# Second SwiGLU of a decoder block: its norm's column sums and broadcast at fixed places, its sums behind the row splits, the gate stage's tiles placed anew

## The chip, the cores and the metric

The kernel runs on one core of one Trainium2 chip. The metric is the device time of one execution in microseconds (us), taken as the median of several runs. A second execution of the same program carries a hardware profile; all rows below come from that one.

The engines are named as the profile names them: PE is TensorE's matmul, PEld its weight load, DVE is VectorE, ACT ScalarE, POOL GpSimd, SP SyncE. L126 is line 126 of the kernel.

## What is computed

One layer of a decoder block on 512 tokens of width 1024. The part that matters here is its end:

```python
h = h + o                                                  # attention + S5, through w_out
h = h + 0.5 * swiglu(rmsnorm(h, norm_ffn2), ffn2_w1, ffn2_w3, ffn2_w2)
gate = sigmoid(rmsnorm(h, norm_ple) @ w_ple_gate)
h = h + gate * (p @ w_ple)                                 # p: 512 x 256, the per-layer embedding
return rmsnorm(h, norm_final)

def swiglu(x, w1, w3, w2): return (silu(x @ w1) * (x @ w3)) @ w2      # d_ff = 2816
def rmsnorm(x, g): return x * rsqrt(mean(x * x, -1) + 1e-6) * g
```

## The kernel before

The state `h` stands with features on the partitions, as a tile of 128 partitions, 8 feature tiles k, 512 tokens. Every large product is made in a reduced float format from split operands: a weight w becomes `hi` (a cast on ACT, L147) and `lo` (raw minus hi, on DVE, L149), an activation likewise `xh` and `xl`, and `mm3` issues three matmuls, hi with xh, hi with xl, lo with xh. Weights come in units of 128 x 1024 (512 KB): `unit()` starts the load on ACT's DMA queue into a ring of four `raw` tiles, and ring places for three `hi` and three `lo` follow. PSUM has four tags A, B, C, D (rows call them ps_A to ps_D) of two banks each; a matmul has to wait until the bank that it writes has been read.

Most of the order of instructions is set by a scheduler, which simulates the program and issues what it thinks will be ready. Two things bind it: `pinned(...)` keeps the marked instructions in the order in which the program gives them, and `tc.issue_after(x)` lets the instructions in its block be placed only behind x. Whatever is left is placed by the scheduler's own simulation. Each engine then works strictly in its order: an instruction that waits holds up everything behind it on that engine.

**From the attention's end to the second SwiGLU.** When `h` is complete, its squares have been added up in `acc` (L183, DVE). The embedding's products p @ w_ple follow on PE: eight feature tiles m, two k tiles each, three matmuls each, 48 in all (rows ps_B<-ph,hi, pl,hi and ph,lo); ACT copies each result (`et`, L1272), and it goes to DRAM for the gate stage. Among these products `rsqrt_rows` makes the norm's factor. Four narrow matmuls sum `acc` over the features (row ps_D<-ones,acc), DVE and POOL work out the reciprocal root (`ms`, `nt`, `ri`, and `dg`, L260 to L267), and one matmul broadcasts it over the partitions (row ps_D<-dg,ones). Only then can `Scaled.spread` make the SwiGLU's input: for each feature tile k, DVE scales the row (`xn`, L218), ACT casts it (`xh`, L219) and DVE subtracts (`xl`, L225). These DVE instructions are pinned among each other. Of the 48 products just the first is pinned, and the sums, the broadcast and the other products stand where the scheduler put them.

**The SwiGLU.** Hidden tiles f are made in turn by `up(f)`. The first two (N_PLAIN = 2), f = 0 and 1, take plain products of 8 k tiles with two weights (j = 0 writes bank A, j = 1 bank B): 2 x 8 x 3 matmuls of 128 x 512 each. From f = 2 on `up_fast` uses a scheme with seven products for eight, of 128 x 256 matmuls, and for it `combine` (in `spread`) makes four sums of quarters of the scaled rows, t1, t2, t4 and t3: two additions on DVE each (L234, rows xn<-xn), a cast on ACT (`sh`, L237), a subtraction on DVE (`sl`, L238). These sums are not pinned and not bound to the splits. The weights of `up_fast` are sums too (`s`, L309 to L316, DVE).

**The gate stage.** After the SwiGLU's last feature tile of `h` (L398) its split and square follow (`xh` L173 and `sq` L182 on ACT, `xl` L174 and `acc` L183 on DVE). The stage goes through the tokens in two halves of 256 and in each through m = 0 to 7, with 24 matmuls of 128 x 256 for each m. Behind m = 0 of the first half come the column sums of `ng.finish`, later the broadcast, a copy of it (`rb`, L192), and with that the first result is scaled (`gt`, L1307); m = 4 needs the bank that the first `gt` reads. The stage's pool `gp` holds the embedding `ple` read back from DRAM, five kept weights `hi` and `lo`, and small tiles. Its tiles share their place in memory with those of the SwiGLU that are freed at its end, so what a gate tile has to wait for depends on where in the pool it lies. `PADS[2]` is a filling of 192 bytes ahead of the tiles that follow.

Of the kernel before, what the change touches and what calls it, by code (L numbers as in the profile page):

```python
# [10 lines left out]
F32 = mybir.dt.float32  # L11
# [8 lines left out]
SEQ = 512  # L20
PLE_DIM = 256
D_FF = 2816
KT = D_MODEL // 128
# [53 lines left out]
def block_kernel(ctx: ExitStack, tc: tile.TileContext, a: dict, out: bass.AP):  # L77
# [73 lines left out]

    def mm3(o, wh, wl, xh, xl, first, last, pin=False):
        p = mm(o, wh, xh, first, False)
        if pin:
            pinned(p)
        mm(o, wh, xl, False, False)
        mm(o, wl, xh, False, last)
        return p

# [34 lines left out]
    class Scaled(Norm):  # L194
# [13 lines left out]
        def spread(self, tmp, xpool, pool, pb):  # L208
# [22 lines left out]
            def combine(n, a, b, op):  # L231
                t = tmp().rearrange("p a (b c) -> p (a b) c", c=256)
                for i in range(2):
                    V.tensor_tensor(t[:, 2 * i:2 * i + 2], a(i), b(i), op)  # L234
                hi = pool.tile([128, 4, 256], FR, name=f"sh{n}")
                lo = pool.tile([128, 4, 256], FR, name=f"sl{n}")
                S.copy(hi, t)  # L237
                V.tensor_tensor(lo, t, hi.bitcast(F32), OP.subtract)  # L238
                return (hi, lo), lambda i: t[:, 2 * i:2 * i + 2]
# [11 lines left out]
    def rsqrt_rows(parts, nb, pin=False):  # L251

        st = bank("D", (128, 4))[:, :nb]
        for b in range(nb):
# [11 lines left out]
        for b in range(nb):  # L266
            V.tensor_scalar(dg[:, b, :], ident, ri[:, b:b + 1], None, OP.mult)  # L267
        pb = bank("D")[:, :nb * 128]
        mm(pb, ones, dg.rearrange("p b t -> p (b t)"), True, True)
        return ri, pb  # L270

# [8 lines left out]
    def ffn(nrm, done, bg=None, first=None, fast=None):  # L280
        wait = next(bg) if bg else None
        with ExitStack() as fctx:
# [74 lines left out]
            def up(f):  # L357
# [6 lines left out]
                if after:  # L364
                    both = [(j, k) for k0 in (0, 4) for j in range(2) for k in range(k0, k0 + 4)]
                for j, k in both:
# [294 lines left out]
    first = unit()  # L661
# [596 lines left out]
    pled = dram.tile([D_MODEL, SEQ], F32, tag="pled", name="pled")  # L1258
    wu = None
    for m in range(KT):  # L1260
# [3 lines left out]
        for k in range(2):  # L1264
            q = (m * 2 + k) % 8
            sl = slice(q * 128, (q + 1) * 128)
            with tc.issue_after(lead.ins) if m + k else nullcontext():
                p = mm3(o, wu[0][:, sl], wu[1][:, sl], ph[:, k], pls[k], k == 0, k == 1, pin=m + k == 0)
            if m + k == 0:
                lead = p  # L1270
        et = fp2.tile([128, SEQ], F32, tag=("t1", "t3")[m % 2], name="et")
        S.copy(et, o)  # L1272
        nc.sync.dma_start(pled[128 * m:128 * m + 128], et)
        if m == 0:
            _, pb2 = rsqrt_rows([n2.acc], 4)
            n2.spread(lambda: hp2.tile([128, 2, SEQ], F32, tag="hq", name="xn"), xpool, x2pool, pb2)
    ffn(n2, feed_next(3), fast=(hp2, fp2))
# [3 lines left out]
    ng = state["n"]  # L1281
    with tc.tile_pool(name="gate", bufs=2, reuse_waits="tile") as gp:
        ple = gp.tile([128, KT, SEQ], F32, tag="ple", name="ple", bufs=1)
        for m in range(KT):
            nc.sync.dma_start(ple[:, m], pled[128 * m:128 * m + 128])
        gf = gp.tile([128, KT], F32, tag="gf", name="gf", bufs=1)
        pad(gp, PADS[2])
        nc.scalar.dma_start(gf, a["gain_f"])
        acc = npool.tile([128, SEQ], F32, tag="acc", name="accf", bufs=1)
        ov = out.rearrange("(k p) t -> p k t", p=128)  # L1290
        HS = SEQ // 2
        gate_w = []
        for hf in range(2):
            cs = slice(hf * HS, hf * HS + HS)
            for i in range(KT):
                m = i if hf == 0 else KT - 1 - i
                if hf == 0:
                    gate_w.append(unit(keep=gp if m < KT - 3 else None))
# [25 lines left out]

N_PLAIN = 2
XSHIFT = 224
FILL = 5
# [10 lines left out]
DEBUG_STOP = None  # L1338
PADS = 320, 0, 192

# [144 lines left out]
```

## Time and profile before

| | us |
|---|---|
| median of 3 runs | 1105.64 |
| lowest, highest | 1103.83, 1106.86 |
| the profiled execution | 1106.72 |
| its span, first to last instruction | 1104.9 |
| PE busy in it | 1054.1 (95%) |
| DVE busy | 776.7 (70%) |
| ACT busy | 462.7 (42%) |
| mean granted clock of TensorE, share of full | 0.973 |

The busy times are sums over the whole span. A row of the timeline gives the start and the length of an instruction; matmuls overlap, so their pace is read from the distance of their starts. A bracket at a row's end is the idle time of that engine just before it, and who ended it. The chain of waits follows the work that ended last back from the end and tells which engine held it for which share.

### The profile page before, as it was taken

To read this page: it belongs to the slowest core of one execution; us is meant where nothing else is said; L and a number is where in the kernel's file an instruction comes from. 1 tells how busy PE (TensorE), PEld (TensorE's weight loads), DVE (VectorE), ACT (ScalarE), POOL (GpSimd) and SP (SyncE) were. 2 spreads that over 40 slices of the span, in tenths; PEclk is the share of its full clock that TensorE was granted. 3 is DMA by queue.
4 is the path that set the end of the run, shared out by engine and by line. 5 is a ranking of instruction groups with operands and counts; after the bars stand their busy time and mean duration, and the time that the engine had idled before them with its cause. 6 is when DMAs were issued, how large, how long until landed. Compare 5 with 4: busy or idle time off the path is not lost.

```text
span 1104.9 us, 15111 instructions
## 1 busy us (share of the span) xinstructions
PE 1054.1 (95%) x5854; PEld 888.6 (80%) x5854; DVE 776.7 (70%) x1328; ACT 462.7 (42%) x786; POOL 164.0 (15%) x187
## 2 busy tenths in 40 slices
PE   7999999999999998888899999899999999999896
PEld 5888888888888887665577667699899899898795
DVE  6995446445447755779688976897598678687766
ACT  6222223124123422236758865455256246255431
POOL 4006146335538100000000000000000000000000
PEclk9999999999999998989799999899999999999898
DMA  7332325327635836557121013233333323325302
GB/s 250 117 114 96 96 96 153 104 94 173 164 96 152 261 113 169 180 173 254 38 71 39 1 39 133 95 96 115 96 97 104 126 80 107 119 77 162 124 2 77
DMA packets 48596, 128.48 MB, mean 116 GB/s; under 512 B 10300, under 2 KB 17052, under 8 KB 47500
## 3 DMA queue, kind: packets, MB, share of 16 engines
q10 hardware_dynamic: 26080, 90.51, 25.6%
q0 software_dynamic: 4336, 17.60, 6.1%
q1 hardware_dynamic: 18108, 19.40, 5.6%
q8 instruction: 46, 0.75, 0.3%
q14 instruction: 26, 0.21, 0.1%
HBM read 111.99 MB, written 15.73 MB: 116 GB/s over the span
## 4 chain that ended last, share of the span: by engine, by line
PE 77%; DVE 8%; DMA 6%; ACT 4%; issue 4%; POOL 0%; SPq 0%; ACTq 0%; POOLq 0%; DVEq 0%
PE ps_C L126 23%; PE ps_A L126 23%; PE ps_B L126 21%; PE ps_D L126 10%; DVE lo L149 1%; DMA kf<-kd 1%; DMA kd<-r 1%; DMA kcd<-ra 1%; DMA qd<-r 1%; DMA qf<-qd 1%; ACT e L737 1%; ACT eh L737 1%; DMA dk<-in_s_dT 1%; DMA cst<-vcd 1%; ACT ps_B L737 1%
## 5 line engine op out<-in xcount | busy, mean ns | idle before, releaser
L147 ACT CAST hi<-raw 128x1024 fp32r<-128x1024 f32 (+2 forms) x148 | 153.7, 1041 | 339.6 <-PE ps_C L126 121.7
L149 DVE TENSOR_TENSOR lo<-raw,hi 128x1024 fp32r<-128x1024 f32 (+2 forms) x148 | 191.0, 1293 | 57.2 <-ACT hi L147 56.5
L126 PE MATMUL ps_C<-hq,hi 128*128 128x512 f32 x704 | 217.2, 390 | 0.7 <-DVE h L398 0.7
L126 PEld LDWEIGHTS ps_C<-hq,hi 128*128 128x128 f32 x704 | 131.4, 188 | 28.2 <-DVE h L398 1.5
L126 PE MATMUL ps_A<-xh,hi 128*128 128x512 f32 (+1 forms) x376 | 133.5, 356 | 9.6 <-ACT xh L173 6.2
L126 PE MATMUL ps_A<-xl,hi 128*128 128x512 f32 (+1 forms) x376 | 133.9, 356 | 5.3 <-DVE xl L225 5.0
L126 PE MATMUL ps_C<-hq,lo 128*128 128x512 f32 x352 | 137.0, 389 | 0.0
L126 PE MATMUL ps_A<-xh,lo 128*128 128x512 f32 (+1 forms) x376 | 132.9, 353 | 0.0
L126 PE MATMUL ps_B<-xh,lo 128*128 128x512 f32 (+1 forms) x280 | 105.2, 376 | 3.7 <-DVE lo L149 3.7
L126 PE MATMUL ps_B<-xh,hi 128*128 128x512 f32 (+1 forms) x280 | 104.8, 374 | 0.1
L126 PE MATMUL ps_B<-xl,hi 128*128 128x512 f32 (+1 forms) x280 | 104.3, 373 | 0.0
L261 POOL TENSOR_TENSOR ri<-ms,negh 128x4 f32<-128x4 f32 (+1 forms) x6 | 5.5, 921 | 594.0 <-DVE ms L260 594.0
L126 PEld LDWEIGHTS ps_A<-xh,hi 128*128 128x128 f32 x376 | 72.5, 193 | 20.4 <-ACT xh L173 6.2
L126 PEld LDWEIGHTS ps_A<-xl,hi 128*128 128x128 f32 x376 | 72.6, 193 | 18.1 <-DVE xl L225 7.7
L398 DVE SCALAR_TENSOR_TENSOR h<-ps_C,h 128x512 f32<-128x512 f32 x64 | 43.9, 689 | 57.2 <-PE ps_C L126 57.0
L147 ACT CAST hi<-s 128x1024 fp32r<-128x1024 f32 x40 | 42.1, 1052 | 92.0 <-PE ps_D L126 39.7
L126 PEld LDWEIGHTS ps_A<-xh,lo 128*128 128x128 f32 x376 | 72.6, 193 | 9.0
L126 PEld LDWEIGHTS ps_C<-hq,lo 128*128 128x128 f32 x352 | 66.1, 188 | 13.7
L126 PEld LDWEIGHTS ps_B<-xh,lo 128*128 128x128 f32 x280 | 54.0, 193 | 13.8 <-DVE lo L149 4.8
L126 PEld LDWEIGHTS ps_B<-xh,hi 128*128 128x128 f32 x280 | 54.1, 193 | 9.6 <-issue 0.5
L149 DVE TENSOR_TENSOR lo<-s,hi 128x1024 fp32r<-128x1024 f32 x40 | 49.0, 1226 | 18.0 <-ACT hi L147 17.9
L126 PEld LDWEIGHTS ps_B<-xl,hi 128*128 128x128 f32 x280 | 54.0, 193 | 9.2 <-issue 0.2
(402 smaller groups left out, 2327.2 us busy)
## 6 DMA issues: line engine op xcount, KB each, us to landing
raw<-in_wpack ACTq DMA_DIRECT2D x168, 512.0 KB, 3.6
sc<-s5d POOLq DMA_DIRECT2D x8, 1024.0 KB, 6.9
raw<-in_wpack SPq DMA_DIRECT2D x4, 512.0 KB, 8.1
h<-in_xT SPq DMA_DIRECT2D x8, 256.0 KB, 4.5
s5d<-fs POOLq DMA_DIRECT2D x1, 2048.0 KB, 11.7
s5d<-gt POOLq DMA_DIRECT2D x1, 2048.0 KB, 12.2
s5d<-tcs POOLq DMA_DIRECT2D x2, 1024.0 KB, 9.5
qf<-qd SPq DMA_DIRECT2D x16, 128.0 KB, 4.4
```

What stands on the lines that cost most here:

```text
L126: return PE.matmul(o, lhsT, rhs, start=start, stop=stop, **kw)
L147: S.copy(hi[:, c], raw[:, c])
L149: V.tensor_tensor(lo[:, c], raw[:, c], hi[:, c].bitcast(F32), OP.subtract)
L261: G.tensor_tensor(ri, ms, negh[:, :nb], OP.pow)
L398: V.scalar_tensor_tensor(h[:, m, :], o, 0.5, h[:, m, :], OP.mult, OP.add)
L737: S.activation(*args, **kw)
```

## The change

It has four parts.

First, all 48 embedding products are pinned, one behind the other, and `rsqrt_rows` is cut in two (`rsqrt_steps`, a generator): the sums with the arithmetic behind them, and the broadcast. `NORM_AT` places the first behind product pair (m, k) = (2, 0), the second behind (4, 1); both matmul groups are pinned in the same row of instructions as the products.

Second, the additions of `combine` are issued only behind the last `xl`.

Third, the products of f = 0 go through k on the outside and j on the inside, where they went through two halves of k with j between.

Fourth, in the gate stage's pool the weights of m = 0 are allocated first, then `gf`, a filling of 24,832 bytes, and then `ple`; `PADS[2]` is 224.

The number of instructions of each engine is the same.

```diff
             def combine(n, a, b, op):
                 t = tmp().rearrange("p a (b c) -> p (a b) c", c=256)
-                for i in range(2):
-                    V.tensor_tensor(t[:, 2 * i:2 * i + 2], a(i), b(i), op)
+                with tc.issue_after(self.last.ins):
+                    for i in range(2):
+                        V.tensor_tensor(t[:, 2 * i:2 * i + 2], a(i), b(i), op)
...
     def rsqrt_rows(parts, nb, pin=False):
+        steps = rsqrt_steps(parts, nb, pin)
+        next(steps)
+        return next(steps)
+
+    def rsqrt_steps(parts, nb, pin=False, pin_last=False):
...
+        yield
         pb = bank("D")[:, :nb * 128]
-        mm(pb, ones, dg.rearrange("p b t -> p (b t)"), True, True)
-        return ri, pb
+        p = mm(pb, ones, dg.rearrange("p b t -> p (b t)"), True, True)
+        if pin_last:
+            pinned(p)
+        yield ri, pb
...
                 if after:
-                    both = [(j, k) for k0 in (0, 4) for j in range(2) for k in range(k0, k0 + 4)]
+                    both = [(j, k) for k in range(KT) for j in range(2)]
...
+    norm2 = rsqrt_steps([n2.acc], 4, True, True)
...
-            with tc.issue_after(lead.ins) if m + k else nullcontext():
-                p = mm3(o, wu[0][:, sl], wu[1][:, sl], ph[:, k], pls[k], k == 0, k == 1, pin=m + k == 0)
-            if m + k == 0:
-                lead = p
+            for i, (w_, x_) in enumerate(((wu[0], ph[:, k]), (wu[0], pls[k]), (wu[1], ph[:, k]))):
+                pinned(mm(o, w_[:, sl], x_, k + i == 0, k == 1 and i == 2))
+            if (m, k) == NORM_AT[0]:
+                next(norm2)
+            if (m, k) == NORM_AT[1]:
+                _, pb2 = next(norm2)
+                n2.spread(lambda: hp2.tile([128, 2, SEQ], F32, tag="hq", name="xn"), xpool, x2pool, pb2)
...
-        if m == 0:
-            _, pb2 = rsqrt_rows([n2.acc], 4)
-            n2.spread(lambda: hp2.tile([128, 2, SEQ], F32, tag="hq", name="xn"), xpool, x2pool, pb2)
...
     with tc.tile_pool(name="gate", bufs=2, reuse_waits="tile") as gp:
+        pad(gp, PADS[2])
+        gate_w = [unit(keep=gp)]
+        gf = gp.tile([128, KT], F32, tag="gf", name="gf", bufs=1)
+        gp.tile([128, PADS[3] // 4], F32, name="gpad", bufs=1)
         ple = gp.tile([128, KT, SEQ], F32, tag="ple", name="ple", bufs=1)
...
-        gf = gp.tile([128, KT], F32, tag="gf", name="gf", bufs=1)
-        pad(gp, PADS[2])
...
-        gate_w = []
...
-                if hf == 0:
+                if hf == 0 and m:
                     gate_w.append(unit(keep=gp if m < KT - 3 else None))
...
+NORM_AT = (2, 0), (4, 1)
...
-PADS = 320, 0, 192
+PADS = 320, 0, 224, 24832
```

What the built programs show of it follows for three places; the lines' numbers have moved by a few between the two kernels.

PE, among the embedding's products (ps_B<-ph and <-pl). The difference has two pieces here, one ahead of the sums and one ahead of the broadcast, with three products taken away in each; the piece at the broadcast reads:

```order
 L126 MATMUL ps_B<-pl,hi 128x512
 L126 MATMUL ps_B<-ph,lo 128x512
-L126 MATMUL ps_B<-ph,hi 128x512
-L126 MATMUL ps_B<-pl,hi 128x512
-L126 MATMUL ps_B<-ph,lo 128x512
 L126 MATMUL ps_D<-dg,ones 128x512
 L126 MATMUL ps_B<-ph,hi 128x512
```

The broadcast stands behind 30 products now and stood behind 36; the sums stand behind 15 and stood behind 18.

DVE, at the row splits of the second SwiGLU, before (`xn<-h` scales a row, `xl` is its split, `xn<-xn` are combine's additions, `sl` its subtraction, `lo<-raw,hi` a weight's split):

```order
L225 TENSOR_TENSOR xl<-xn,xh 128x512
L218 SCALAR_TENSOR_TENSOR xn<-h,gains,ps_D 128x512
L234 TENSOR_TENSOR xn<-xn 128x512 x2
L225 TENSOR_TENSOR xl<-xn,xh 128x512
L218 SCALAR_TENSOR_TENSOR xn<-h,gains,ps_D 128x512
L234 TENSOR_TENSOR xn<-xn 128x512
L225 TENSOR_TENSOR xl<-xn,xh 128x512
L238 TENSOR_TENSOR sl<-xn,sh 128x1024
L234 TENSOR_TENSOR xn<-xn 128x512 x2
L225 TENSOR_TENSOR xl<-xn,xh 128x512
L149 TENSOR_TENSOR lo<-raw,hi 128x1024 x2
```

The same place now, on from the fifth split:

```order
L222 TENSOR_TENSOR xl<-xn,xh 128x512
L215 SCALAR_TENSOR_TENSOR xn<-h,gains,ps_D 128x512
L222 TENSOR_TENSOR xl<-xn,xh 128x512
L215 SCALAR_TENSOR_TENSOR xn<-h,gains,ps_D 128x512
L222 TENSOR_TENSOR xl<-xn,xh 128x512 x2
L232 TENSOR_TENSOR xn<-xn 128x512 x2
L149 TENSOR_TENSOR lo<-raw,hi 128x1024 x2
L232 TENSOR_TENSOR xn<-xn 128x512 x2
L149 TENSOR_TENSOR lo<-raw,hi 128x1024
L236 TENSOR_TENSOR sl<-xn,sh 128x1024
```

Five additions and one subtraction went from between the splits to behind the last one; two additions and then two weight splits stand there first.

ACT, at the change from the SwiGLU to the gate stage, before (`xh` and `sq` are of the last feature tiles of h, `hi` the gate weights' casts):

```order
L173 ACTIVATE xh<-h,gains 128x512
L182 ACTIVATE sq<-h 128x512
L1288 DMA gf<-in_gain_f 128x8
L173 ACTIVATE xh<-h,gains 128x512
L182 ACTIVATE sq<-h 128x512
L147 CAST hi<-raw 128x1024 x4
```

And now:

```order
L170 ACTIVATE xh<-h,gains 128x512
L179 ACTIVATE sq<-h 128x512
L147 CAST hi<-raw 128x1024
L1297 DMA gf<-in_gain_f 128x8
L170 ACTIVATE xh<-h,gains 128x512
L179 ACTIVATE sq<-h 128x512
L147 CAST hi<-raw 128x1024 x3
```

One cast went ahead of the last `xh` and `sq`. On DVE the `lo` that belongs to it went ahead of the last `xl` and `acc` in the same way.

## Rows read from the trace of the kernel before

**Rows 1.** The profile's page: the span, the busy times of PE, and the chain of waits by engine.

```profile
span 1104.9 us, 15111 instructions
...
PE 1054.1 (95%) x5854; PEld 888.6 (80%) x5854; DVE 776.7 (70%) x1328; ACT 462.7 (42%) x786; POOL 164.0 (15%) x187
...
PE 77%; DVE 8%; DMA 6%; ACT 4%; issue 4%; POOL 0%; SPq 0%; ACTq 0%; POOLq 0%; DVEq 0%
```

**Rows 2.** The waits of PE, from 660 to 720 us (the norm and the first hidden tiles of the second SwiGLU): engine and what it worked on, whom it waited for, us in total, times, the longest.

```profile
PE ps_A L126 <- DVE xl L225: 5.0, 5, 2.0
```

**Rows 3.** Busy time by windows: the row splits, and a stretch of the SwiGLU later. Columns: window, its length, busy us of each engine (with the number of instructions), TensorE's granted clock as a share of full, DMA share, GB/s.

```profile
685.00:699.00 14.00, 8.93 (x30) 5.09 (x29) 13.43 (x21) 7.68 (x11) 0.00 (x0) 0.93 0.10 38
900.00:1000.00 100.00, 100.00 (x735) 95.20 (x735) 80.43 (x117) 46.60 (x76) 0.00 (x0) 1.00 0.35 107
```

**Rows 4.** The timeline of DVE from 671 to 713 us: start, length, line, operation, what it writes and reads.

```profile
674.02 0.68 DVE L183 TENSOR_TENSOR acc<-acc,sq 128x512 f32<-128x512 f32 x1
...
678.87 0.88 DVE L267 TENSOR_SCALAR dg<-ident,ri 128x128 f32<-128x128 f32 x4
682.38 1.41 DVE L218 SCALAR_TENSOR_TENSOR xn<-h,gains,ps_D 128x512 f32<-128x512 f32 x2 [2.63 <-PE ps_D L126]
...
689.52 0.69 DVE L225 TENSOR_TENSOR xl<-xn,xh 128x512 fp32r<-128x512 f32 x1
...
690.78 1.29 DVE L234 TENSOR_TENSOR xn<-xn 128x512 f32<-128x512 f32 x2
...
693.25 0.69 DVE L234 TENSOR_TENSOR xn<-xn 128x512 f32<-128x512 f32 x1
...
694.45 1.22 DVE L238 TENSOR_TENSOR sl<-xn,sh 128x1024 fp32r<-128x1024 f32 x1
695.58 1.29 DVE L234 TENSOR_TENSOR xn<-xn 128x512 f32<-128x512 f32 x2
696.79 0.69 DVE L225 TENSOR_TENSOR xl<-xn,xh 128x512 fp32r<-128x512 f32 x1
697.39 2.36 DVE L149 TENSOR_TENSOR lo<-raw,hi 128x1024 fp32r<-128x1024 f32 x2
```

**Rows 5.** The timeline of ACT in the same stretch.

```profile
684.91 1.05 ACT L147 CAST hi<-raw 128x1024 fp32r<-128x1024 f32 x1
...
686.34 1.14 ACT L219 CAST xh<-xn 128x512 fp32r<-128x512 f32 x2
```

**Rows 6.** The timeline of PE from the embedding's products to the first 128 x 256 product of `up_fast`.

```profile
675.29 0.39 PE L126 MATMUL ps_B<-ph,hi 128*128 128x512 f32 x1
...
675.98 0.95 PE L126 MATMUL ps_D<-ones,acc 128*128 128x1 f32 x8
...
679.42 0.39 PE L126 MATMUL ps_B<-ph,lo 128*128 128x512 f32 x1
...
681.32 1.02 PE L126 MATMUL ps_D<-dg,ones 128*128 128x512 f32 x2
...
692.73 0.50 PE L126 MATMUL ps_A<-xl,hi 128*128 128x512 f32 x1 [1.49 <-DVE xl L225]
...
697.53 0.80 PE L126 MATMUL ps_A<-xl,hi 128*128 128x512 f32 x1 [1.98 <-DVE xl L225]
698.12 0.63 PE L126 MATMUL ps_A<-xh,lo 128*128 128x512 f32 x1
...
703.95 0.41 PE L126 MATMUL ps_B<-xh,lo 128*128 128x512 f32 x1
...
716.69 0.28 PE L126 MATMUL ps_A<-xh,hi 128*128 128x256 f32 x1
```

**Rows 7.** Busy time by windows of 2 us from the last row split on, columns as in rows 3.

```profile
696.00:698.00 2.00, 0.47 (x1) 0.47 (x2) 2.00 (x4) 1.05 (x1) 0.00 (x0) 0.79 0.00 0
698.00:700.00 2.00, 2.00 (x5) 1.18 (x5) 2.00 (x3) 1.62 (x2) 0.00 (x0) 0.50 0.22 33
```

**Rows 8.** The timeline of PE at the gate stage.

```profile
1039.45 0.58 PE L126 MATMUL ps_A<-xh,hi 128*128 128x256 f32 x1 [2.99 <-ACT hi L147]
...
1045.53 0.95 PE L126 MATMUL ps_D<-ones,acc 128*128 128x1 f32 x8
...
1053.54 1.02 PE L126 MATMUL ps_D<-dg,ones 128*128 128x512 f32 x2
...
1055.90 0.36 PE L126 MATMUL ps_A<-xh,hi 128*128 128x256 f32 x1 [0.28 <-DVE gt L1307]
```

**Rows 9.** The timeline of DVE at the gate stage.

```profile
1036.49 0.69 DVE L398 SCALAR_TENSOR_TENSOR h<-ps_C,h 128x512 f32<-128x512 f32 x1 [0.56 <-PE ps_C L126]
...
1039.43 4.63 DVE L149 TENSOR_TENSOR lo<-raw,hi 128x1024 fp32r<-128x1024 f32 x4
...
1054.60 0.69 DVE L192 COPY rb<-ps_D 128x512 f32<-128x512 f32 x1 [2.18 <-PE ps_D L126]
```

**Rows 10.** The timeline of ACT at the gate stage.

```profile
1034.45 0.62 ACT L182 ACTIVATE sq<-h 128x512 f32<-128x512 f32 x1
...
1038.37 2.93 ACT L147 CAST hi<-raw 128x1024 fp32r<-128x1024 f32 x3
```

**Rows 11.** Busy time by a window of 2 us at the gate stage's start, columns as in rows 3.

```profile
1038.00:1040.00 2.00, 0.55 (x2) 0.50 (x2) 1.90 (x3) 2.00 (x3) 0.00 (x0) 0.62 0.00 0
```

**Rows 12.** DMA issues from 690 to 715 us: what, queue, count, KB each, median us from issue to landing.

```profile
raw<-in_wpack ACTq DMA_DIRECT2D x5, 512.0 KB, 3.7
```

More of the change, by code (lines that the diff above doesn't have):

```diff
@@ L150, in split, with mm3 @@
         return hi, lo
[L152 to L155, printed above, removed]
+    def mm3(o, wh, wl, xh, xl, first, last):
+        mm(o, wh, xh, first, False)
         mm(o, wh, xl, False, False)
         mm(o, wl, xh, False, last)
-        return p
     xpool = ctx.enter_context(tc.tile_pool(name="xpool", bufs=1))
@@ L1258, in block_kernel @@
     pled = dram.tile([D_MODEL, SEQ], F32, tag="pled", name="pled")
-    wu = None
+    norm2 = rsqrt_steps([n2.acc], 4, True, True)
     for m in range(KT):
```

## The prediction

> **What bounds the kernel now.** I read the page first. PE is busy for 1054.1 of 1104.9 us and holds 77% of the chain of waits [rows 1]; so the kernel can only gain where PE waits or where it runs slowly. The profiled execution took 1106.72 us, 1.8 us more than its span, and lies 0.1% over the median of 1105.64; I work on its rows and take the difference off the median.
>
> Second, PE's waits around the change. From 660 to 720 us there are five waits for a row split `xl`, 5.0 us together [rows 2]. The window of the splits shows why: from 685 to 699 us DVE works 13.43 of 14.00 us and PE only 8.93 [rows 3]. DVE is the bound there. Later in the SwiGLU the same row view has PE full and DVE at 80% [rows 3]: there, time won at the start is kept, and DVE work put off from the splits finds room. A difference under 0.3%, 3.3 us, can hardly be told from none.
>
> Third, the granted clock. PE waits 1.98 us for the last split, after a stretch in which it was about half busy [rows 3, 6]. [...] The products from 698.12 to 703.95 run in 13 steps of 0.448 us, against 0.2275 in the 56 steps from 703.95 to 716.69 [rows 6]. The slow stretch costs 13 x 0.22 = **2.9 us**. The gate stage has the same picture: PE idles 2.99 us for a weight cast [rows 8], the clock is 0.62 from 1038 to 1040 [rows 11], and 26 products take 6.08 us up to the column sums at 1045.53 [rows 8].
>
> **Part 1, sums and broadcast.** Three products are 675.98 - 675.29 = 0.69 us [rows 6]; the sums start that much earlier, at 675.29. `acc` is complete at 674.02 + 0.68 = 674.70 [rows 4], so no wait is added. The chain through DVE and POOL ended with `dg` at 678.87 + 0.88 = 679.75 [rows 4] and ends now at 679.06. The broadcast's new place, behind 30 products, comes up at 679.42 + 0.23 = 679.65 [rows 6], 0.6 us later than `dg`: PE does not wait, and queued behind it would only be products that nobody awaits soon. It stood at 681.32, so it comes **1.67 us** earlier, and the first scaled row starts at 680.71, not at 682.38 [rows 4]. The embedding's results are needed only in the gate stage, 350 us later; that six products come after the broadcast costs nothing, since PE works through the same 48 in the same time. SP's and POOL's queues keep their order.
>
> **Part 2, the sums of quarters.** Between the splits DVE did five additions and one subtraction. By the distance to the next row's start, a pair of additions took 696.79 - 695.58 = 1.21 us, the subtraction 695.58 - 694.45 = 1.13 [rows 4]: 5 x 0.60 + 1.13 = **4.1 us** leave the path. One thing is late next: ACT's weight cast at 684.91 waits for the embedding's last product, whose time does not move, and the fourth `xh` stands behind it and a copy, at 686.34 [rows 5]. So the fourth split cannot start before about 686.95, where its turn would be at 685.9: about 1.0 us is lost, of which 0.5 had been lost before. From there, at a pace of 1.26 (689.52 to 690.78 [rows 4]), splits five to seven start at 688.21, 689.47 and 690.73, the eighth at 691.47; it ends at 692.16. It ended at 696.79 + 0.69 = 697.48 [rows 4]: **-5.3 us**, which agrees with -1.7 - 4.1 + 0.5.
>
> **Part 3, the loop order, and PE behind the splits.** With j inside, each split feeds six products of f = 0 instead of three as soon as both weights are there, so PE has more to do between splits. Its waits for splits four to six come to 0.4, 0.5 and 0.5 us in the replay. Behind the last split two new ones arise, because the two additions now stand ahead of the weight splits on DVE (they were 697.39, directly behind the last split [rows 4]): a weight's `lo` is done at 694.6, for which PE waits 0.4 us, and PE waits 1.1 us for a cast `hi` whose place in the ring comes free late. Both are bounded by 0 and by the whole pair of additions with a cast, 1.2 + 1.05 = 2.3 us [rows 4, 5]; I take **+1.5**, the replay's own value. No single wait in it comes near the 1.98 or 2.99 us after which the clock fell, and the half-busy stretch is half as long; I therefore count the 2.9 us of slow clock as gone. Sum for the norm: -5.3 - 2.9 + 1.5 = **-6.7 us**; the first 128 x 256 product moves from 716.69 to about 710.0.
>
> [...]
>
> **Part 4, the gate stage.** The cast of m = 0 now stands ahead of the last `xh` and `sq` on ACT; it starts when the square before is done, 1034.45 + 0.62 = 1035.07 [rows 10], and ends at 1036.1. Its `lo` follows the last `h` on DVE, 1036.49 + 0.60 = 1037.09 [rows 9], and ends at 1038.3. PE can do its first two products at once, then waits about 1.7 us for `lo`, and goes on at 1038.38 where it went on at 1039.45 [rows 8]. If the clock stays up, 24 products at the full pace follow. That pace is (1053.54 - 1045.53 - 0.81) / 61 = 0.118 us for the 61 products between sums and broadcast [rows 8]; 0.81 is the time the sums take up. So the sums start at 1041.2 instead of 1045.53, **-4.3 us**: 1.1 from the earlier start, 0.2 from two products done earlier, 3.0 from the clock. The last `xl` and `acc` move back by one `lo`, 1.2 us; `acc` is ready at 1039.5, before it is needed. The broadcast stands behind three products fewer: 1041.2 + 0.81 + 58 x 0.118 = 1048.85 against 1053.54 [rows 8]. Then one step is lost again. `rb` follows 1.06 later, as before (1054.60 [rows 9]), at 1049.9, but one `lo` (4.63 / 4 = 1.16 us a piece [rows 9]) now stands on DVE between it and the first `gt`, so `gt` starts at 1051.7 and m = 4 on PE at 1052.2, with a wait of 1.1 us where it had 0.28. It started at 1055.90 [rows 8]: **-3.7 us**. From there on both kernels run the same rows.
>
> **Sum.** -6.7 - 3.7 = -10.4 us: the profiled execution would be 1096.3, the median **1095.2**. With no new wait behind the splits (-1.5) and none at `gt` (-1.1) it is 1092.6.
>
> **The rivals.** (a) The clock falls all the same. For it: PE is only half to two thirds busy from 684 to 692 us, and at the gate a wait of 1.7 us stands close to the 1.98 that was followed by a fall. Against it: in 685 to 699 the mean clock was still 0.93 although PE worked 8.93 of 14 us, so half-busy alone did not bring it down [rows 3], and a wait of 1.49 us passed without a fall [rows 6]. At the norm it costs 2.9 (1098.1), at the gate 2.7 (1097.9; 3.0 for the products, less what the wait at `gt` takes up), at both 1100.8.
>
> (b) The put-off sums come too late. DVE has no idle time between 692 and about 711 us in my replay: six more rows of it lie behind the splits, and the first weight sum of `up_fast` needs a load that lands 3.7 us after issue [rows 12]. The third subtraction is ready at 710.3, PE needs it at 713.2: 2.9 us of slack. A missed ring place costs one landing and one cast, 3.7 + 1.05, less the slack: 2 to 3 us, or about 1098.
>
> (c) The gate's cast gets no earlier, since its place in memory still has a reader among the last products. Then only the norm counts: 1098.9.
>
> (d) Slower. The same queue of DVE work as in (b) at one place, the sums for f = 2: PE stops there until the last one is made. It decides from a lateness of 2.9 + 10.4 = 13.3 us on, that is two to three loads missed one behind the other at 4.75 each beyond the slack; over 1109 it needs 16.6. DVE's 80% in the later window [rows 3] speaks against any such pile-up.
>
> **How the numbers follow.** Forecast 0.66; (a) 0.17; (b) 0.09; (c) 0.06; (d) 0.02. The predicted time is the forecast's, 1095. The range goes from 1092, where none of the new waits arises, to 1101, where the clock falls at both places; outside lie (d) and combinations of (a) to (c), under 2 in 10. Faster by more than 3.3 us: all of the forecast and nearly all of (a) to (c), 0.93; within: 0.05, combinations; slower: 0.02.
>
> **What would show it.** In the profile after: the broadcast at about 679.7 with no wait ahead of it on PE; eight `xl` rows on DVE with no addition between them, the last ending near 692; no stretch of clock 0.50 between 690 and 705; the first 128 x 256 product near 710. At the gate: one weight cast ahead of the last `xh`, sums some 11 us earlier than 1045.53, the clock at 1.00. I am wrong if the clock falls, if PE has a new wait for `sl`, `sh` or `s` near 703 to 715, or if DVE becomes the bound over the first products of `up_fast`.

## The result and the profile after

The changed kernel takes 1092.87 us in the median of 4 runs (1090.99 to 1096.34), before 1106.13 on the same chip (4 runs, 1103.83 to 1106.86): 13.3 us less. The ratio of the two means is 0.9887, with a 95% interval from 0.9856 to 0.9918: 1.13% or 12.5 us less, at least 9.1 and at most 15.9. Predicted were 1095 and a range from 1092 to 1101.

The profile page of the changed kernel has the span, the busy times and the chain of waits in the lines that answer to [rows 1]:

```profile
span 1089.1 us, 15119 instructions
...
PE 1042.0 (96%) x5854; PEld 881.4 (81%) x5854; DVE 775.2 (71%) x1328; ACT 462.1 (42%) x786; POOL 163.9 (15%) x187
...
PE 78%; DVE 8%; DMA 5%; issue 4%; ACT 4%; SPq 0%; POOLq 0%; POOL 0%; ACTq 0%; DVEq 0%
```

The profiled execution is 15.8 us shorter in its span. This is not yet the change's work: the stretches have to be cut out. Two marks that both traces have are the embedding's first product on PE and the first 128 x 256 product of the second SwiGLU; I call the time between their starts the norm's segment. A second pair is the last 128 x 512 product of the SwiGLU (ps_C) and the first product of m = 4, which is the first one on bank A behind the broadcast; the time between these I call the gate segment.

PE's timeline of the changed kernel, norm's segment:

```profile
666.51 0.39 PE L126 MATMUL ps_B<-ph,hi 128*128 128x512 f32 x1
...
669.98 0.95 PE L126 MATMUL ps_D<-ones,acc 128*128 128x1 f32 x8
...
674.35 1.02 PE L126 MATMUL ps_D<-dg,ones 128*128 128x512 f32 x2
...
686.18 0.50 PE L126 MATMUL ps_A<-xl,hi 128*128 128x512 f32 x1 [0.30 <-DVE xl L222]
...
688.60 0.50 PE L126 MATMUL ps_B<-xh,hi 128*128 128x512 f32 x1 [0.90 <-ACT hi L147]
...
689.29 0.50 PE L126 MATMUL ps_B<-xh,lo 128*128 128x512 f32 x1
...
704.38 0.28 PE L126 MATMUL ps_A<-xh,hi 128*128 128x256 f32 x1
```

The norm's segment is 704.38 - 666.51 = **37.87 us** here, and it was 716.69 - 671.82 = 44.87 before, 671.82 being the start of that product in the trace of before: 7.00 us less. The sums stand 3.47 us behind the start, where they stood 4.16; the broadcast 7.84, where it stood 9.50 [rows 6]. No bracket stands at either, so neither had to be waited for. DVE's timeline of the same stretch:

```profile
675.41 1.41 DVE L215 SCALAR_TENSOR_TENSOR xn<-h,gains,ps_D 128x512 f32<-128x512 f32 x2 [1.66 <-PE ps_D L126]
...
681.65 0.69 DVE L222 TENSOR_TENSOR xl<-xn,xh 128x512 fp32r<-128x512 f32 x1 [0.94 <-ACT xh L216]
...
685.44 1.46 DVE L222 TENSOR_TENSOR xl<-xn,xh 128x512 fp32r<-128x512 f32 x2
686.82 1.29 DVE L232 TENSOR_TENSOR xn<-xn 128x512 f32<-128x512 f32 x2
688.02 2.35 DVE L149 TENSOR_TENSOR lo<-raw,hi 128x1024 fp32r<-128x1024 f32 x2
```

The first scaled row starts 1.06 us behind the broadcast, as before. The fourth split waits at 681.65, 0.94 us, for its `xh`, which is the hold behind ACT's cast; ACT's timeline has that cast and, behind a copy, the fourth and the fifth `xh`:

```profile
679.57 1.05 ACT L147 CAST hi<-raw 128x1024 fp32r<-128x1024 f32 x1 [0.24 <-PE ps_B L126]
...
681.00 1.14 ACT L216 CAST xh<-xn 128x512 fp32r<-128x512 f32 x2
```

The last two splits stand together at 685.44 and end at 686.90, 20.39 us behind the segment's start, where it was 25.66 [rows 4]: 5.27 us earlier. Only then come two additions and two weight splits. What PE still waits for, from 660 to 715 us (columns as in rows 2):

```profile
PE ps_B L126 <- ACT hi L147: 0.9, 1, 0.9
PE ps_A L126 <- DVE xl L222: 0.8, 3, 0.3
```

Five waits of 5.0 us [rows 2] have become three short ones of 0.8 us and one new wait of 0.9 for a cast. The windows about the splits (columns as in rows 3) show the clock at full, where it was at half for some 7 us before [rows 6, 7]:

```profile
684.00:686.00 2.00, 1.58 (x6) 0.67 (x4) 2.00 (x4) 1.06 (x2) 0.00 (x0) 1.00 0.00 0
686.00:688.00 2.00, 1.51 (x5) 0.78 (x5) 1.92 (x4) 0.68 (x2) 0.00 (x0) 1.00 0.00 0
688.00:690.00 2.00, 1.41 (x5) 0.92 (x6) 2.00 (x3) 1.97 (x3) 0.00 (x0) 1.00 0.00 0
```

PE's timeline at the gate stage:

```profile
1023.83 0.40 PE L126 MATMUL ps_C<-hq,lo 128*128 128x512 f32 x1
...
1026.15 0.38 PE L126 MATMUL ps_A<-xh,lo 128*128 128x256 f32 x1 [1.68 <-DVE lo L149]
...
1029.06 0.95 PE L126 MATMUL ps_D<-ones,acc 128*128 128x1 f32 x8
...
1036.72 1.02 PE L126 MATMUL ps_D<-dg,ones 128*128 128x512 f32 x2
...
1040.08 0.36 PE L126 MATMUL ps_A<-xh,hi 128*128 128x256 f32 x1 [0.94 <-DVE gt L1315]
```

and DVE's:

```profile
1024.88 1.22 DVE L149 TENSOR_TENSOR lo<-raw,hi 128x1024 fp32r<-128x1024 f32 x1
...
1037.77 0.69 DVE L189 COPY rb<-ps_D 128x512 f32<-128x512 f32 x1 [0.88 <-PE ps_D L126]
1038.38 1.22 DVE L149 TENSOR_TENSOR lo<-raw,hi 128x1024 fp32r<-128x1024 f32 x1
1039.51 0.42 DVE L1315 TENSOR_TENSOR gt<-ps_A,rb 128x256 f32<-128x256 f32 x1
```

The last 128 x 512 product of the SwiGLU starts at 1023.83 in this trace, at 1036.07 in that of before. The sums come 5.23 us behind it (9.46 before), the broadcast 12.89 (17.47), m = 4 16.25 (19.83): the **gate segment is 3.58 us shorter**. The 2.99 us for a cast [rows 8] have become 1.68 us for a `lo`, and the clock behind them is the full one (a window of 2 us, columns as in rows 3), where it was at 0.62 in the window about the cast before [rows 11]:

```profile
1026.00:1028.00 2.00, 1.85 (x15) 1.86 (x16) 2.00 (x4) 2.00 (x3) 0.00 (x0) 1.00 0.43 78
```

At 1040.08 the new wait of 0.94 us stands: between `rb` at 1037.77 and `gt` at 1039.51 DVE makes a weight's `lo`.

The two segments give 7.00 + 3.58 = 10.6 us of the profiled 15.8. Between them both traces agree to 0.1 us (319.38 and 319.45), and behind the gate segment too (49.00 and 49.04). The other 5.3 us lie ahead of the embedding's first product: 671.82 against 666.51. Up to it the two programs have the same instructions in the same order on each engine, so this is the spread of single executions, not the change. Over the 14 profiles of this study that mark lies between 666.36 and 671.82, with either kernel's order at both ends. It goes with the clock: ahead of the mark the granted clock was at half for 38 us in all in the trace of before and for 24 us in that of the changed kernel. In the two profiles with 38 us the mark lies at 671.8, in the five with 34 at 668.1 to 671.0, in the seven with 31 or less at 666.4 to 667.7.

### The profile page after: what moved, and what is told of

Its sections match the earlier page's. It is cut to its first block, busy times and chain, and to the rows that moved or that the text cites. A ratio compares the mean times of both kernels' runs of the same rounds, so it can differ in the third digit from the quotient of the medians.

```text
span 1089.1 us, 15119 instructions
## 1 busy us (share of the span) xinstructions
PE 1042.0 (96%) x5854; PEld 881.4 (81%) x5854; DVE 775.2 (71%) x1328; ACT 462.1 (42%) x786; POOL 163.9 (15%) x187
## 4 chain that ended last, share of the span: by engine, by line
PE 78%; DVE 8%; DMA 5%; issue 4%; ACT 4%; SPq 0%; POOLq 0%; POOL 0%; ACTq 0%; DVEq 0%
PE ps_C L126 24%; PE ps_A L126 23%; PE ps_B L126 21%; PE ps_D L126 10%; DMA kf<-kd 1%; DVE nmax L1053 1%; DMA kd<-r 1%; DVE lo L149 1%; DMA qd<-r 1%; ACT e L743 1%; DMA qf<-qd 1%; ACT eh L743 1%; ACT ps_B L743 1%; DMA cst<-vcd 1%; DVE el L1148 0%
## 5 line engine op out<-in xcount | busy, mean ns | idle before, releaser
L149 DVE TENSOR_TENSOR lo<-s,hi 128x1024 fp32r<-128x1024 f32 x40 | 49.0, 1225 | 16.5 <-ACT hi L147 15.8
```

The lines of the kernel that those rows point to most:

```text
L149: V.tensor_tensor(lo[:, c], raw[:, c], hi[:, c].bitcast(F32), OP.subtract)
```

## Experiments

### The parts one by one

The third part needs no run: with the old loop or the new one, the built programs are the same, instruction for instruction on each engine, both in the kernel before and in the changed one. The scheduler places these products by what it expects to be ready, and writes the same row from either loop.

The other parts were run alone and left out. `places_alone` is the kernel before with the first part:

```diff
+    norm2 = rsqrt_steps([n2.acc], 4, True, True)
...
+                pinned(mm(o, w_[:, sl], x_, k + i == 0, k == 1 and i == 2))
+            if (m, k) == NORM_AT[0]:
+                next(norm2)
+            if (m, k) == NORM_AT[1]:
+                _, pb2 = next(norm2)
...
```

> The kernel before with part 1 alone (sums behind 15 products, broadcast behind 30, all pinned). Measured from the embedding's first product to the first 128x256 product: 44.87 us before, 37.87 in the changed kernel. My theory (the splits end when DVE is through with splits and additions, and one wait of about 2 us then drops the clock): the broadcast is 1.67 earlier, the hold of the fourth xh takes 0.4 back, the additions stay between the splits and the clock falls as before: 43.5 us, the time about 1.3 us under before. Rival (the earlier broadcast alone shortens the last wait enough to keep the clock): 40.6 us. Rival (places give nothing, the order behind them decides): 44.9. Gate segment, from the last 128x512 product of the SwiGLU to m = 4: unchanged at 19.8.

`sums_behind_alone` is the kernel before with the second:

```diff
-                for i in range(2):
-                    V.tensor_tensor(t[:, 2 * i:2 * i + 2], a(i), b(i), op)
+                with tc.issue_after(self.last.ins):
+                    for i in range(2):
+                        V.tensor_tensor(t[:, 2 * i:2 * i + 2], a(i), b(i), op)
```

> The kernel before with part 2 alone (combine's additions behind the last split, products at their old places). Theory: the last split ends 4.1 us earlier, no single wait reaches 1.9 us, the clock stays up (2.9), two new waits take 1.5 back: 39.4 us in the segment of 44.87, the time about 5.5 us under before. Rival (half-busy PE between the splits drops the clock by itself): 42.3 us in the segment. Gate segment 19.8.

`gate_alone` is the kernel before with the fourth:

```diff
+        pad(gp, PADS[2])
+        gate_w = [unit(keep=gp)]
+        gf = gp.tile([128, KT], F32, tag="gf", name="gf", bufs=1)
+        gp.tile([128, PADS[3] // 4], F32, name="gpad", bufs=1)
         ple = gp.tile([128, KT, SEQ], F32, tag="ple", name="ple", bufs=1)
...
-PADS = 320, 0, 192
+PADS = 320, 0, 224, 24832
```

> The kernel before with part 4 alone (the gate pool's tiles placed anew). Theory: the norm's segment stays at 44.9 us; at the gate the cast stands ahead, PE waits 1.7 us for lo and the clock stays at full: 16.3 us from the last 128x512 product to m = 4, against 19.83 before; time 3.6 us under before. Rival (the clock was saved there by something else in the changed kernel): clock 0.5 to 0.6 behind the wait and 18.8 us.

`without_sums_behind` is the changed kernel without the second part, the additions outside of `issue_after` again:

```diff
-                with tc.issue_after(self.last.ins):
-                    for i in range(2):
-                        V.tensor_tensor(t[:, 2 * i:2 * i + 2], a(i), b(i), op)
+                for i in range(2):
+                    V.tensor_tensor(t[:, 2 * i:2 * i + 2], a(i), b(i), op)
```

> The changed kernel without part 2 (combine's additions free again). Theory: the additions come back between the splits, a wait of about 2 us and the slow clock with them: 43.5 us in the norm's segment (37.87 with part 2), gate segment 16.3 as in the changed kernel; time about 5.6 us over the changed kernel. Rival (places carry the gain, the additions find room): 38 to 39 us in the segment.

`norm_only` is the changed kernel with the gate pool as before (the fourth part's diff turned round).

> The changed kernel with the gate stage's tiles as before. Theory: norm's segment 37.9 us as in the changed kernel, gate segment 19.8 as before with the clock at half behind the wait of 3.0 us; time 3.6 us over the changed kernel, 7.0 under before. Rival (the gate's wait and clock come from the earlier arrival of the SwiGLU, not from the tiles): gate segment 16 to 17 us.

Measured; the segments are distances of starts in each trace, the last split's end is counted from the norm's segment's start, and the ratio is to the kernel before on the same chip:

| kernel | last split ends | norm's segment | gate segment | ratio (95% interval) |
|---|---|---|---|---|
| before | 25.66 | 44.87 | 19.83 | 1 |
| places_alone | 24.37 | 42.51 | 18.97 | 0.9987 (0.9969 to 1.0006) |
| sums_behind_alone | 21.68 | 39.17 | 18.58 | 0.9950 (0.9931 to 0.9969) |
| gate_alone | 25.66 | 44.74 | 16.13 | 0.9986 (0.9972 to 1.0000) |
| without_sums_behind | 24.37 | 42.48 | 15.86 | 0.9967 (0.9947 to 0.9986) |
| norm_only | 20.39 | 37.87 | 18.79 | 0.9927 (0.9904 to 0.9950) |
| changed | 20.39 | 37.87 | 16.25 | 0.9887 (0.9856 to 0.9918) |

The last split goes as worked out: 1.29 us from the places, 3.98 from the sums of quarters, 5.27 from both. The second part carries most: alone it takes 5.7 us out of the norm's segment and is faster beyond its interval. The places alone give 2.4 us there where 1.4 were expected, and a time that cannot be told from none. Their trace has the fall of the clock too, but sooner, 21.7 us behind the segment's start instead of 25.3, among the waits, where it costs less: behind the last split the segment is 1.1 us shorter than before. Without the second part the segment of the changed kernel is 4.6 us longer (5.6 expected), and the clock falls. The gate's tiles work in either surrounding: with them the gate segment is 15.86 to 16.25 us, without them 18.58 to 19.83. The rival that the earlier arrival saves the gate's wait falls with `norm_only`, where PE waits for the cast as before:

```profile
1027.76 0.39 PE L126 MATMUL ps_A<-xh,hi 128*128 128x256 f32 x1 [2.99 <-ACT hi L147]
...
1028.71 0.39 PE L126 MATMUL ps_B<-xh,hi 128*128 128x256 f32 x1 [0.45 <-ACT hi L147]
```

and where the clock falls behind it:

```profile
1028.00:1030.00 2.00, 1.55 (x12) 1.34 (x12) 2.00 (x2) 2.00 (x3) 0.00 (x0) 0.97 0.06 10
1030.00:1032.00 2.00, 2.00 (x11) 2.00 (x11) 2.00 (x3) 0.56 (x1) 0.00 (x0) 0.50 0.94 268
```

The gate segment without the new tiles is not a fixed number. In the four kernels with this stage as it was, all with the wait of 2.99 to 3.00 us, it was 19.83, 18.97, 18.58 and 18.79 us. The clock fell 2.4, 4.6, 3.6 and 5.5 us behind the start of the SwiGLU's last product, and it stayed at half for some 7 us in before, for some 3 us in the other three. With the new tiles the segment lay between 15.86 and 16.25, so the part is worth 2.3 to 4.0 us by these rows, some 3.0 in the mean, rather than the 3.58 of the one pair. In time `gate_alone` gave 1.5 us (0 to 3.1), less than the 3.6 expected, which lies outside that interval; the mean of the rows is just inside.

### What brings the clock down

The prediction held that one long wait drops the clock and that being half busy does not. `gate_alone` already speaks against it. Its instructions in the norm's segment are those of before, and so are its waits. PE's waits for splits there:

```profile
687.34 0.50 PE L126 MATMUL ps_A<-xl,hi 128*128 128x512 f32 x1 [1.50 <-DVE xl L225]
...
689.20 0.80 PE L126 MATMUL ps_A<-xl,hi 128*128 128x512 f32 x1 [0.80 <-DVE xl L225]
...
692.14 0.80 PE L126 MATMUL ps_A<-xl,hi 128*128 128x512 f32 x1 [1.29 <-DVE xl L225]
```

The windows of the same stretch:

```profile
686.00:688.00 2.00, 0.67 (x3) 0.49 (x3) 2.00 (x5) 1.21 (x3) 0.00 (x0) 1.00 0.00 0
688.00:690.00 2.00, 1.20 (x4) 0.71 (x3) 2.00 (x3) 0.59 (x1) 0.00 (x0) 0.51 0.00 0
690.00:692.00 2.00, 0.85 (x2) 0.13 (x1) 2.00 (x5) 1.05 (x1) 0.00 (x0) 0.50 0.00 0
...
698.00:700.00 2.00, 2.00 (x9) 1.60 (x9) 2.00 (x3) 0.52 (x1) 0.00 (x0) 0.93 0.20 49
```

The clock is down from about 688 us, right behind the wait of 1.50 us and 21.6 us behind the segment's start. In the trace of before it stood at full through the same wait (1.49 us, [rows 6]) and fell 3.7 us later. The segment took 44.74 us here and 44.87 there, though the clock was at half for some 10 us instead of some 7: what falls into the time in which PE waits for DVE anyway costs nothing more.

Three kernels then put superfluous 128 x 512 operations on DVE ahead of the splits, in the changed kernel; they write a tile that nothing reads any more, so the output stays as it is:

```diff
+                for _ in range(3 if k == KT else 0):
+                    pinned(V.scalar_tensor_tensor(self.acc, h[:, 0, :], gains[:, self.gi, 0:1], pb, OP.mult, OP.mult))
                 if k:
                     self.last = pinned(V.tensor_tensor(self.xl[:, k - 1], row(k - 1),
```

That is `one_wait_short`; `one_wait_long` has 6 in place of 3, and `many_waits` one ahead of each of the last six splits (`range(1 if k > 2 else 0)`). Each of the three was run once (1094.63, 1097.4 and 1100.1 us; before took 1104.04 in the median on that chip), so each reading of the clock below is of a single execution. Theory 1 is that one wait of about 2 us is enough; theory 2 that it takes such a wait and a half-busy stretch ahead of it; the rival that short waits are enough.

> The changed kernel with three superfluous 128x512 operations on DVE (each about 0.66 us, they write a tile that is not read) ahead of the last split only. PE then has one wait of about 1.8 us for the last split, and before it is three quarters busy instead of half. Theory 1 (one wait of near 2 us is enough to drop the clock): segment 37.9 + 2.0 + 2.9 = 42.8 us, clock 0.5 for some 6 us behind the wait. Theory 2 (the fall needs the wait and the half-busy stretch ahead of it together): 39.9 us, clock 1.00.

> The changed kernel with six such operations ahead of the last split: one wait of about 3.8 us. Theories 1 and 2 both: the clock falls, since 2.99 us at the gate were followed by a fall with PE full ahead of it; segment 37.9 + 4.0 + 2.9 = 44.8 us. If the clock stays at 1.00: 41.8 us, and both fall.

> The changed kernel with six such operations, one ahead of each of the last six splits: the same 4.0 us of DVE time, spread over waits of 0.9 to 1.2 us each, PE about 40% busy over some 11 us. Theories 1 and 2 (a long single wait is needed): clock 1.00, segment 41.8 us. [...]

| kernel | waits for splits | last split ends | norm's segment | clock |
|---|---|---|---|---|
| changed | 0.22, 0.30, 0.30 | 20.39 | 37.87 | 1.00 |
| one_wait_short | 0.22, 0.29, 0.30, 1.86 | 22.44 | 41.50 | falls |
| one_wait_long | 0.22, 0.30, 0.30, 4.21 | 24.78 | 44.50 | falls |
| many_waits | 0.94, 0.95, 0.95 | 23.14 | 42.35 | falls |

In `many_waits` PE has no wait over 0.95 us:

```profile
689.86 0.51 PE L126 MATMUL ps_A<-xl,hi 128*128 128x512 f32 x1 [0.94 <-DVE xl L224]
...
691.78 0.50 PE L126 MATMUL ps_A<-xl,hi 128*128 128x512 f32 x1 [0.95 <-DVE xl L224]
...
693.70 0.79 PE L126 MATMUL ps_A<-xl,hi 128*128 128x512 f32 x1 [0.95 <-DVE xl L224]
```

and its clock falls all the same, at the end of the third:

```profile
690.00:692.00 2.00, 1.05 (x4) 0.57 (x5) 2.00 (x4) 0.62 (x1) 0.00 (x0) 1.00 0.00 0
692.00:694.00 2.00, 1.05 (x4) 0.57 (x4) 2.00 (x4) 0.62 (x1) 0.00 (x0) 0.92 0.00 0
694.00:696.00 2.00, 2.00 (x5) 1.04 (x4) 2.00 (x4) 0.19 (x1) 0.00 (x0) 0.50 0.00 0
```

In `one_wait_short` it falls at about 691.4, behind the single wait of 1.86 us that ended at 689.16 and the wait of 0.90 for the cast that the changed kernel has too:

```profile
686.00:688.00 2.00, 1.00 (x4) 0.48 (x3) 1.93 (x4) 0.33 (x1) 0.00 (x0) 1.00 0.00 0
688.00:690.00 2.00, 0.73 (x2) 0.30 (x2) 2.00 (x4) 0.31 (x1) 0.00 (x0) 1.00 0.00 0
690.00:692.00 2.00, 1.21 (x3) 0.80 (x4) 2.00 (x3) 1.98 (x3) 0.00 (x0) 0.85 0.00 0
692.00:694.00 2.00, 2.00 (x6) 1.52 (x6) 2.00 (x4) 1.77 (x3) 0.00 (x0) 0.50 0.75 213
```

In `one_wait_long` the clock stayed at full for the first 4.0 us of the wait of 4.21 us, from 686.99 to 691.20, and fell 0.2 us before its end:

```profile
688.00:690.00 2.00, 0.00 (x0) 0.00 (x0) 1.89 (x4) 0.00 (x0) 0.00 (x0) 1.00 0.00 0
690.00:692.00 2.00, 0.80 (x2) 0.50 (x2) 2.00 (x4) 0.00 (x0) 0.00 (x0) 0.75 0.00 0
```

So the one long wait of theory 1 is not needed, since `many_waits` has none. Theory 2, which wants such a wait too, falls by the same run, and it forecast a full clock for `one_wait_short`. That run does not show what the wait of 1.86 us does alone, since the fall came only behind the second wait. What the rows leave is the rival: in `many_waits` the clock fell at the end of the third of three waits of 0.94 to 0.95 us, 1.92 us apart, in one execution. Shorter ones were not followed by a fall: 0.22 to 0.30 us and one of 0.90 in the changed kernel, and 0.28 to 0.30 us and one of 0.91 in `sums_behind_alone`. What PE did before the fall can be read from the windows: it was busy for 1.06, 1.05 and 1.05 of 2 us in `many_waits` (the first of them from 688 to 690), for 1.00 and 0.73 in `one_wait_short`; in the changed kernel for 1.58, 1.51 and 1.41, and there the clock stayed up. The time at which it falls is not fixed by the instructions, as `gate_alone` against before shows: 21.6 and 25.3 us behind the segment's start. In the changed kernel no fall came, and the norm gave 7.00 us.

The fall cost less than the 2.9 us of before in all three. `one_wait_short` is 3.63 us longer than the changed kernel, with a last split 2.05 later: 1.6 us are left for the clock, if nothing else behind the split changed. In `many_waits` it is 4.48 with 2.75, in `one_wait_long` 6.63 with 4.39: 1.7 and 2.2. The clock was at half for some 3 us in the first and for some 7 in the other two, as in before.

### What is left

Four more runs on one chip: the changed kernel again, and three versions that take away its own waits. `changed_again` is the changed kernel itself.

> The changed kernel once more, on the chip of the two that follow. Norm's segment 37.9 us, gate segment 16.2, clock 1.00 in both, as in its first profile; time 9 to 12 us under before. If the clock falls in one of them in this run, the gain of the clock is not safe from run to run.

`gt_first` puts the eighth gate weight's `lo` behind the first `gt`:

```diff
-                    gate_w.append(unit(keep=gp if m < KT - 3 else None))
+                    gate_w.append(unit(keep=gp if m < KT - 3 else None, after=first_gt if m == KT - 1 else None))
...
-                V.tensor_tensor(t, o, ng.rb[:, cs], OP.mult)
+                gt = V.tensor_tensor(t, o, ng.rb[:, cs], OP.mult)
+                if hf == 0 and i == 0:
+                    first_gt = gt
```

> The changed kernel with the eighth gate weight's lo behind the first gt instead of ahead of it. If that lo holds up gt, as the rows of the changed kernel say (0.94 us of PE's wait), the gate segment goes from 16.25 to 15.3 us. If PE's wait comes from rb instead, it stays at 16.2.

`f0_first` adds to that a fixed order for f = 0 and f = 1 on PE, and the second weight's `lo` ahead of the sums:

```diff
+                if after:
+                    nrm.sums(lo_ins[0])
...
+                    for k in range(KT):
+                        sl = slice(k * 128, (k + 1) * 128)
+                        for j in range(2):
+                            pinned(mm(z[j], wu[j][0][:, sl], nrm.xh[:, k, :], k == 0, False))
+                            pinned(mm(z[j], wu[j][0][:, sl], nrm.xl[:, k, :], False, False))
+                            if j == 0:
+                                pinned(mm(z[0], wu[0][1][:, sl], nrm.xh[:, k, :], False, k == KT - 1))
+                    for k in range(KT):
+                        sl = slice(k * 128, (k + 1) * 128)
+                        pinned(mm(z[1], wu[1][1][:, sl], nrm.xh[:, k, :], False, k == KT - 1))
...
```

> gt_first, and at the norm: f = 0 takes both weights' hi products with each split and all lo products of the second weight at the end, f = 1 strictly behind f = 0, and the second weight's lo ahead of the sums of quarters instead of behind two of them. What the changed kernel still waits for there is 0.2 + 0.3 + 0.3 us for splits, 0.9 for a cast that two products of f = 1 placed too early bring in, and 0.1 for that lo. With five products for each split PE needs 1.14 us against DVE's 1.26, so these waits shrink to some 0.5 us: segment 37.9 to about 36.5 us (only the waits), or 35 if the sums are not late. Rival: two 128x256 products of f = 2 now stand ahead of f = 1 and wait for their weight's cast: a new wait of 1 to 3 us, segment 37 to 40. Gate 15.3.

`f0_first_behind` keeps f = 2 behind f = 1:

```diff
-                product(zx[:, lo], u0, 0, nrm.quarter(0, 0), True)
+                with tc.issue_after(f1_last[0].ins) if f == 2 else nullcontext():
+                    product(zx[:, lo], u0, 0, nrm.quarter(0, 0), True)
```

> f0_first with the products of f = 2 kept strictly behind those of f = 1. The run f0_first had one wait of 1.04 us for a cast ahead of two 128x256 products that stood too early, and 0.3 us for a copy later. If these are all that is left, the stretch from the embedding's first product to the last 128x512 product of the SwiGLU goes from 356.6 us (357.3 in the changed kernel) to about 355.3, the norm's segment to 35.9, the gate segment stays at 15.2, and the time comes 2 to 3 us under the changed kernel. Rival (the wait moves: DVE's sums are now late for f = 2, a wait for sl or lo of 1 to 2 us): 356.5.

Measured; the second column goes from the embedding's first product to the SwiGLU's last 128 x 512 product, since two 128 x 256 products change places in `f0_first`. All four ran on the same chip, the last one at another time:

| kernel | to the SwiGLU's end | gate segment | median us | lowest to highest | ratio to before (95% interval) |
|---|---|---|---|---|---|
| before | 364.25 | 19.83 | 1104.18 (11 runs) | 1099.50 to 1106.14 | 1 |
| changed_again | 357.30 | 16.27 | 1091.87 (5) | 1089.35 to 1094.30 | 0.9891 (0.9871 to 0.9912) |
| gt_first | 357.37 | 15.26 | 1092.65 (5) | 1092.28 to 1093.88 | 0.9904 (0.9888 to 0.9919) |
| f0_first | 356.63 | 15.15 | 1090.74 (6) | 1088.74 to 1093.59 | 0.9887 (0.9868 to 0.9906) |
| f0_first_behind | 355.30 | 15.16 | 1091.15 (6) | 1088.92 to 1093.51 | 0.9886 (0.9864 to 0.9908) |

(The two segments of before are those of its one profile. At the time of `f0_first_behind` before took 1103.98 us, 11 runs.) `changed_again` repeats both segments to 0.02 us, with the clock at 1.00 in both. The `lo` ahead of `gt` is shown to cost 1.0 us: in `gt_first` the wait is gone. In `f0_first` all waits for splits are gone, but the rival came true in small; PE's waits from 665 to 740 us:

```profile
PE ps_A L126 <- ACT hi L148: 1.0, 1, 1.0
PE ps_A L126 <- ACT p L343: 0.3, 1, 0.3
```

The 1.0 us is the wait ahead of the two early products. In `f0_first_behind` only the second is left:

```profile
PE ps_A L126 <- ACT p L344: 0.3, 1, 0.3
```

By its trace that kernel is 2.0 us shorter at the norm and 1.1 at the gate than the changed one, as expected; its median is 0.7 us lower. That is inside the spread of single runs, 1.6 us in `gt_first` and some 5 us in each of the others: all three versions beat the kernel before, and none is shown to beat the changed kernel in time.

## Why the prediction was right, and where its reasons were not

**Part 1.** Right in every step: the broadcast came 1.66 us earlier (1.67 worked out), and PE did not have to wait at either group of pinned matmuls.

**Part 2.** The last split ended 5.27 us earlier (5.3), with the hold of the fourth split where it was expected and of the size expected. `sums_behind_alone` and `without_sums_behind` confirm that this part carries the norm's gain.

**Part 3.** This step failed. The prediction had each split feed six products because j went inside; the loop changes nothing in the program. What lets PE run ahead behind the splits is the order that the scheduler wrote in any case, with f = 0's first weight ahead, a few products of other weights between, and the rest at the end. The waits were a little smaller than in the prediction's replay, of which it gives only the results: 0.2, 0.3 and 0.3 us for splits (0.4, 0.5, 0.5), 0.9 for the cast (1.1), and 689.29 stands 0.13 later than at full pace for the `lo` (0.4). Both kernels have 70 products behind the last split in the segment; they took 19.21 us and take 17.48. With 2.9 us for the slow clock, the term of +1.5 measured about +1.2, and the norm's sum -7.0 instead of -6.7.

**The clock.** The result was forecast, the reason was wrong. The slow stretch of before went, as predicted: in both profiles of the changed kernel, in `norm_only` and in `gt_first`, which have its order at the splits, the clock stayed at 1.00. But that no wait came near 1.98 us was no reason for it; waits of 0.95 us were enough for a fall. Nor did the fall of before come after the wait of 1.98 us: 0.79 over the window from 696 to 698 us [rows 7] puts it at about 697.2, inside that wait, which ended at 697.53. At the gate 0.62 [rows 11] puts it at about 1038.5, 1.0 us before the end of the 2.99. What closed in the changed kernel was not only the last wait but all of them, 5.0 us down to 0.8. The chance of 0.17 for rival (a) was therefore argued from the wrong rows. Its evidence against, that half-busy alone had not brought the clock down by 697 us, is undone by `gate_alone`, where the same stretch did so 3.7 us sooner. Which of the waits, or how much idle time in all, decides is not shown.

**Part 4.** Right step by step: sums 4.23 us earlier (4.3), broadcast 4.58 (4.7), m = 4 3.58 (3.7), the wait for `lo` 1.68 (1.7) and the one at `gt` 0.94 (1.1). Only the size of what it replaces was taken from one execution; over four kernels the old gate segment is 0.8 us shorter in the mean.

**The rivals.** (b), the late sums, did not happen: PE has no wait for `sl`, `sh` or `s` in the stretch from 660 to 715 us. (c) fell with the one cast ahead of the last `xh`, and (d) with (b).

**The sum.** Forecast -10.4, in the rows -10.6, in the medians -13.3 on the first chip and -12.3 on the one of `changed_again`. The intervals of both hold -10.6. That forecast and rows agree to 0.2 us is in part luck: the gate's 3.58 us stand against the longest of the four old gate segments, and with the mean of 3.0 the rows give -10.0. Whether the remaining 2 us of the medians are the spread ahead of the embedding or something that the segments don't show is not settled; the programs give no reason for the second.

## What to carry to other kernels

An instruction that nobody awaits, placed between steps that everybody awaits, cost its whole length here (the last split ended 3.98 us earlier without the 4.1 us of sums ahead of it): look on the bound engine for work that could stand behind the last awaited row, and check what is queued behind it (here a cast, 0.9 us). When an engine waits in many small pieces for another, the price is the waits and possibly the clock as well, so closing them can give back more than they last (here 5.0 us of waits became 1.7, and the norm's segment 7.00 us shorter). A stretch at the slow clock is to be priced over several executions: its length changed from one to the next (some 7 us in before, some 10 in `gate_alone`, with the same instructions). Before costing an edit of a loop under a scheduler, see whether the built order changes at all.

## What the runs showed of the hardware

The granted clock of TensorE went from 1.00 of full to 0.50 at the end of the third of three waits of 0.94 to 0.95 us (`many_waits`), behind one of 1.86 and one of 0.90 us (`one_wait_short`), 4.0 us into one of 4.21 us (`one_wait_long`), and with the same instructions at times 3.7 us apart (`gate_alone` and before). At the gate it stayed up through a wait of 1.68 us in all ten profiles with the new tiles. It fell in all four without them, from 1.0 us before the end of the wait of 2.99 to 3.00 us to 2.1 us behind it. A fall cost 1.6 to 2.2 us in the three kernels with delays, not the 2.9 us of before, and a stretch of some 10 us at half among waits cost no more than one of some 7 (segments of 44.74 and 44.87 us).
